# A two-layer block with routed experts: places turned with their weights in them, outputs gated as they leave, the general path moved to the end

## The chip, the cores and the metric

One core of a Trainium2 chip runs the whole program in one launch. The metric is device time in microseconds (us). Engines: PE is the matrix engine (PEld its weight loads), DVE the vector engine, ACT the scalar engine, POOL the GpSimd, SP the queue that issues nearly all loads. PE's clock is granted at one of two levels, 1.2 and 2.4 GHz; the profile gives it as a share of the higher.

## The reference, cut to what matters

256 tokens of width 1024 go through two layers. A layer has a token mixer (three branches, untouched here) and then a mixture of 16 experts in 4 groups, of which each token uses two of one group:

```
x  = x + g_a * token_mixer(...)
hf = rmsnorm(x, ffn_norm) * (1 + sc_f) + sh_f
lg, le = hf @ w_rg + b_rg, hf @ w_re + b_re            # group and expert logits
g      = argmax(lg);  top two experts inside group g   # (the first at a tie)
w2     = softmax(top two) * softmax(lg)[g]
combine[token, expert] = w2 at its two experts, else 0
hid    = silu(hf @ w_gate[e]) * (hf @ w_up[e]) * combine
x      = x + g_f * sum_e hid[e] @ w_down[e]
```

Products are float32. Weights of the dense part are split in a high and a low part (fp32r) and multiplied in three passes.

## The kernel before, in words

Tokens lie in two blocks of 128 (t = 0, 1). At the end of the mixer the w_out product comes in two halves of columns (hf) and two blocks. For each, `residual` (L1046) adds to x, sums its squares on ACT (L1055), turns it on PE (L1059) and multiplies it with the router's weights (L1068). `logits` (L1072) makes the norm's factor and the logits, and on ACT the high part xh of the normed tokens (L1081). `place` (L1084) finds the two experts of each token on DVE in a chain of small passes that ends in E (L1092), counts on PE which place the token gets among its expert's (L1095), and writes the place matrix Sm (L1102): token by expert by 32 places, one where the token sits. Behind it come the low parts xl, on DVE (L1105). The residual of block 1, half 1, is ordered behind E of block 0 (L1053).

`gather` (L1112) multiplies xh and xl with Sm: each expert gets a block of 2 x 32 token places. Each result is moved from PSUM by ACT, or by DVE for every second one of block 1.

Experts go in eight pairs q, two at once on the two halves of PE's columns. `gate_up(q)` (L1185) is 32 matmul instructions on four loads of 1 MB; `hidden` (L1199) makes silu times up on DVE and multiplies with cs[:, q], the weight of the token at each place; `turned_hidden` (L1207) turns that on PE, ACT copies it; `down` (L1215) is 16 instructions in two halves of columns on two more loads, and `split` (L108) writes its result as a high part on ACT and a low part on DVE (L109). `scatter` (L1291) multiplies the turned places ST with these two parts, in PSUM sums acc[t][hf] over all experts. PE's order in the loop is gate_up(q+1), scatter(q-1), down(q), turn of q+1; `queued` (L1179) fixes it.

Between gate_up(0) and gate_up(1) stand: the count of tokens that found no place (L1261), the weights by place, as 32 instructions that multiply Sm's columns with the combine weights (L1276) and two copies to cs (L1279), and 16 transposes of Sm (L1284), four to a PSUM bank, copied to ST by ACT (L1285). The combine weights come from DVE and ACT (Exp at L1237, L1238, then L1239 on), in free gaps that the scheduler finds.

`overfull` (L375) is the general path for tokens without a place: a branch on a flag, not taken with this input. It stands before down(7); every engine reads the flag (L377) and branches (L378). In its body it adds to acc.

`last_add` (L1326) multiplies acc by the gate g_f (rows[:, 1]) and adds it to x: in layer 0 inside the next layer's norm (L436), in layer 1 before the stores (L1335).

Loads: `pump` (L203) takes them in one fixed order whenever a buffer is put back to one of the pools wa, fs, rs; SP issues them in that order.

## Time and profile before

| | us |
|---|---|
| median of 3 runs | 837.86 (836.51 to 838.67) |
| profiled execution | 837.31 |
| its span, first to last instruction | 835.5 |
| PE busy | 788.2 (94%) |
| DVE busy | 539.5 (65%) |
| ACT busy | 387.0 (46%) |
| POOL busy | 30.0 (4%) |

The experts' part runs from 304.3 to 420 in layer 0 and from 714.6 to 829 in layer 1. A row of the timeline has its start, its length, the engine, the line, what is written and read, the count, and in brackets the idle time before it and what ended it. A row of a table by stretches has its limits, its length, the busy time (and count) of PE, PEld, DVE, ACT and POOL, the granted clock, the share of the DMA engines and GB/s. A row by lines has the busy time, the mean of one in ns, and the idle time before.

### The profile page before, as it was taken

Reading aid. Unit: us, or ns where it says so; the run is one execution under the profiler, and the core shown is the slowest. Engines: PE = TensorE matmul, PEld = TensorE weight load, DVE = VectorE, ACT = ScalarE, POOL = GpSimd, SP = SyncE. Lnnn points to the kernel's source line nnn. Section 1 sums busy time; section 2 is a strip of 40 time slices with the busy share of each in tenths; the row PEclk is TensorE's granted clock in tenths of the full one; section 3 lists DMA queues with packets and bytes.
Section 4 is the critical chain, followed back from the end, with each engine's and each line's share of the span. In section 5 each row is a group of like instructions: output and inputs, shape, how many; then the busy total and the mean of one; then the engine's idle time right before and its main releaser. Section 6 shows DMA issues by size and latency. Waiting matters only on the chain. (4 is left out here: it accounts for less than half of the span.)

```text
span 835.5 us, 11106 instructions
## 1 busy us (share of the span) xinstructions
PE 788.2 (94%) x3836; PEld 550.4 (66%) x3836; DVE 539.5 (65%) x1384; ACT 387.0 (46%) x855; POOL 30.0 (4%) x60
## 2 busy tenths in 40 slices
PE   4999999999999889999869999999999997999996
PEld 2876877788887755333358687887888885633332
DVE  6889889888999641111288987998557757211113
ACT  5477747654455242111267674776555444311111
POOL 0103001000000000000000300000000000000001
PEclk9999999999999988999979998999999997899999
DMA  9975745789899558999726366668977446599981
GB/s 340 407 299 167 269 169 200 310 312 374 320 416 371 197 198 343 422 420 422 283 108 231 115 270 249 214 244 318 356 264 254 142 152 252 201 370 420 420 349 51
DMA packets 36109, 234.37 MB, mean 281 GB/s; under 512 B 4017, under 2 KB 4689, under 8 KB 10450
## 3 DMA queue, kind: packets, MB, share of 16 engines
q1 hardware_dynamic: 35410, 231.52, 71.9%
q0 software_dynamic: 576, 2.10, 0.7%
q8 instruction: 31, 0.51, 0.2%
q14 instruction: 28, 0.23, 0.1%
q10 hardware_dynamic: 64, 0.02, 0.0%
HBM read 232.55 MB, written 1.06 MB: 280 GB/s over the span
## 5 line engine op out<-in xcount | busy, mean ns | idle before, releaser
L472 PE MATMUL mm<-rs,rs 128*128 128x512 f32 (+1 forms) x432 | 173.2, 404 | 5.5 <-ACT rs L563 4.9
L365 ACT ACTIVATE rs<-wa 128x512 fp32r<-128x512 f32 (+1 forms) x224 | 135.4, 633 | 90.9 <-PE mm L473 68.9
L473 PE MATMUL mm<-rs,rs 128*128 128x512 f32 (+1 forms) x432 | 175.2, 406 | 0.1
L474 PE MATMUL mm<-rs,rs 128*128 128x512 f32 (+1 forms) x432 | 174.8, 405 | 0.0
L365 DVE TENSOR_TENSOR rs<-wa,rs 128x512 fp32r<-128x512 f32 (+1 forms) x224 | 148.5, 682 | 39.3 <-ACT rs L365 25.0
L284 DVE SCALAR_TENSOR_TENSOR wa<-wa,cb 128x1024 f32<-128x1024 f32 x90 | 107.9, 1214 | 0.0
L472 PEld LDWEIGHTS mm<-rs,rs 128*128 128x128 f32 x432 | 82.9, 193 | 22.3 <-ACT rs L563 6.2
L473 PEld LDWEIGHTS mm<-rs,rs 128*128 128x128 f32 x432 | 83.6, 194 | 16.7 <-DVE rs L564 1.1
L474 PEld LDWEIGHTS mm<-rs,rs 128*128 128x128 f32 x432 | 83.7, 194 | 15.7 <-issue 1.4
L1203 DVE SCALAR_TENSOR_TENSOR th<-th,mm 128x256 f32<-128x256 f32 x16 | 6.7, 421 | 98.2 <-ACT th L1202 98.1
L109 DVE TENSOR_TENSOR fs<-mm,fs 128x512 fp32r<-128x512 f32 x32 | 22.1, 691 | 63.6 <-ACT fs L109 63.6
L1195 PE MATMUL mm<-wa,xs 128*64 128x512 f32 x160 | 58.5, 603 | 0.0
L1195 PE MATMUL mm<-fs,xs 128*64 128x512 f32 x192 | 58.3, 603 | 0.0
L1202 ACT ACTIVATE th<-mm 128x256 f32<-128x256 f32 x16 | 6.1, 384 | 105.6 <-PE mm L1195 105.6
L109 ACT ACTIVATE fs<-mm 128x512 fp32r<-128x512 f32 x32 | 19.1, 597 | 69.8 <-PE mm L1224 69.8
L1195 PE MATMUL mm<-rs,xs 128*64 128x512 f32 x160 | 42.8, 595 | 0.0
L472 PE MATMUL mm<-rs,xs 128*128 128x512 f32 x96 | 37.6, 392 | 0.0
L474 PE MATMUL mm<-rs,xs 128*128 128x512 f32 x96 | 37.5, 391 | 0.0
L473 PE MATMUL mm<-rs,xs 128*128 128x512 f32 x96 | 37.4, 390 | 0.0
L1195 PEld LDWEIGHTS mm<-wa,xs 128*64 128x64 f32 x160 | 17.2, 139 | 29.7 <-issue 29.7
L1224 PE MATMUL mm<-fs,hid 128*64 128x512 f32 x104 | 32.8, 598 | 1.6 <-DVEq L378 1.6
L365 ACT ACTIVATE rs<-fs 128x512 fp32r<-128x512 f32 x40 | 23.8, 627 | 21.0 <-PE mm L473 14.8
(334 smaller groups left out, 1309.3 us busy)
## 6 DMA issues: line engine op xcount, KB each, us to landing
wa<-in_ws_dram SPq DMA_DIRECT2D x83, 1024.0 KB, 7.0
fs<-in_ws_dram SPq DMA_DIRECT2D x47, 1024.0 KB, 10.2
wa<-in_wada_dram SPq DMA_DIRECT2D x40, 1024.0 KB, 5.0
rs<-in_ws_dram SPq DMA_DIRECT2D x30, 1024.0 KB, 12.3
wa<-in_wada_dram SPq DMA_DIRECT2D x10, 512.0 KB, 10.5
wa<-in_ws_dram SPq DMA_DIRECT2D x6, 512.0 KB, 8.8
fs<-in_wada_dram SPq DMA_DIRECT2D x6, 512.0 KB, 9.7
fs<-row POOLq DMA_DIRECT2D x4, 512.0 KB, 6.9
```

The source lines that it names most:

```text
L109: return ACT.activation(h, src, AF.Copy), DVE.tensor_tensor(l, src, h.bitcast(F32), op=OP.subtract)
L284: DVE.scalar_tensor_tensor(w, w, 0.5, cb, op0=OP.mult, op1=OP.mult, accum_out=mods[l][:, 2 * i + j:2 * i + j + 1])
L365: pinned(ACT.activation(h[:, cs_], r[:, cs_], AF.Copy), DVE.tensor_tensor(lo[:, cs_], r[:, cs_], h[:, cs_].bitcast(F32), op=OP.subtract))
L472: PE.matmul(o, ah[:, kb + k, ts], hv[:, k], start=st, stop=False)
L473: PE.matmul(o, al[:, kb + k, ts], hv[:, k], start=False, stop=False)
L474: PE.matmul(o, ah[:, kb + k, ts], lv[:, k], start=False, stop=en)
L1195: queued(PE.matmul(pgu[64 * i:64 * i + 64], a, wv[i][:, k], start=kb == 0, stop=kb == 7))
L1202: ACT.activation(th, pgu[:, :256], AF.Tanh, scale=0.5)
L1203: DVE.scalar_tensor_tensor(th, th, 1.0, pgu[:, :256], op0=OP.add, op1=OP.mult)
L1224: queued(PE.matmul(py[hf][i_], hid_[:, f, i_], wv[i][:, f, hs], start=f == 0, stop=f == 1))
```

## The change

The weight matmuls go. Sm holds only the block's own places and lies in the buffer that ST takes later (so it is taken earlier, before place(0)); a second matrix Sw, Sm times the combine weights with the zeros of the other block, is made on DVE and turned. A sum over a row of the turned matrix is the weight at that place (cs), and a comparison with zero gives ST. Four transposes make one group; groups 0 and 1 stand between gate_up(0) and gate_up(1), groups 2 and 3 and the count behind gate_up(1) and the turn of hidden 0. `down` multiplies its result by the gate before it is split, into the row buffer of the other gate, and `last_add` only adds. `overfull` comes after the last scatter; in its body the down weights are multiplied by the gate. The low parts of block 0 are made by an ACT copy and a GpSimd subtraction. The first two passes of the combine weights are ordered behind the low parts of block 1.

```diff
-        def overfull(acc, cov, ovi):
+        def overfull(acc, cov, ovi, gate):
...
+                    for f in range(2):
+                        DVE.tensor_tensor(wv[:, f], wv[:, f], gate, op=OP.mult)
...
-        xh_s, xl_s, sm_s = (fs.get(F32R) for _ in range(3))
+        xh_s, xl_s = (fs.get(F32R) for _ in range(2))
+        sw_s = fs.get()
...
-        Sm = sm_s.rearrange("p (t e u s) -> p t e u s", t=2, e=16, u=2)
+        Sw = sw_s.rearrange("p (t e u s) -> p t e u s", t=2, e=16, u=2)
         for t in range(2):
-            POOL.memset(Sm.bitcast(F32)[:, t, :, 1 - t], 0.0)
+            POOL.memset(Sw[:, t, :, 1 - t], 0.0)
...   # logits
             for hs in halves:
                 ACT.activation(xh[:, t, hs], x[:, t, hs], AF.Copy, scale=r)
+            if t == 0:
+                for hf, hs in enumerate(halves):
+                    xn = tm_s[:, 1024 * hf:1024 * hf + 512]
+                    ACT.activation(xn, x[:, t, hs], AF.Copy, scale=r)
+                    POOL.tensor_tensor(xl[:, t, hs], xn, xh[:, t, hs].bitcast(F32), op=OP.subtract)
...   # place
-            for hs in halves:
-                o = DVE.scalar_tensor_tensor(xl[:, t, hs], x[:, t, hs], rstd[t], xh[:, t, hs].bitcast(F32), ...)
-                behind_of(o, placed)
+            if t:
+                for hs in halves:
+                    o = DVE.scalar_tensor_tensor(xl[:, t, hs], x[:, t, hs], rstd[t], xh[:, t, hs].bitcast(F32), ...)
+                    behind_of(o, placed)
+                order["xl"] = o
...
         logits(0)
-        place(0)
         for s, kb, hv, lv in todo:
             mm3(ps[1], kb, 8, hv, lv, mh, ml, 1)
             rs.put(s)
         rs.put(mh_s, ml_s)
+        st_s = rs.get()
+        Sm = st_s[:, :1024].rearrange("p (t e s) -> p t e s", t=2, e=16)
+        ST = st_s.rearrange("p (q t n) -> p q t n", q=8, t=2)
+        place(0)
         residual(1, 1, ps[1])
         logits(1)
-        xs.put(tm_s, hT_s)
+        xs.put(hT_s, tm_s)
         gather(0, 0, 4)
         place(1)
         gather(0, 4)
-        st_s = rs.get()
-        ST = st_s.rearrange("p (q t n) -> p q t n", q=8, t=2)
...   # down
-                split(y_s[:, hs], y_s[:, 1024 + 512 * hf:1536 + 512 * hf], py[hf])
+                y = rows_s[:, hs]
+                DVE.tensor_tensor(y, py[hf], rows[:, 1, hs], op=OP.mult)
+                split(y_s[:, hs], y_s[:, 1024 + 512 * hf:1536 + 512 * hf], y)
...
-        pgu = gate_up(0)
+        pgs = [gate_up(0)]
...   # both first passes of the combine weights
+        behind_of(DVE.tensor_tensor(ex, ...), order["xl"])
+        behind_of(DVE.tensor_tensor(d, ...), order["xl"])
...
+        for t in range(2):
+            DVE.tensor_tensor(Sw[:, t, :, t], Sm[:, t].bitcast(F32), cmb[:, t, :, None].to_broadcast([128, 16, 32]), op=OP.mult)
+        cs = small("cs", 8)
+
+        def turned_places(g):
+            p = mmt("sm").rearrange("p (q t n) -> p q t n", q=2, t=2)
+            for i in range(2):
+                for t in range(2):
+                    e = 2 * (2 * g + i)
+                    queued(PE.transpose(p[:, i, t], Sw[:, t, e:e + 2].rearrange("p e u s -> p (e u s)"), ident))
+            g2 = slice(2 * g, 2 * g + 2)
+            DVE.tensor_reduce(cs[:, g2], p.rearrange("p q t n -> p q (t n)"), axis=AX.X, op=OP.add)
+            DVE.tensor_scalar(ST[:, g2], p, 0.0, None, op0=OP.is_gt)
+
+        for g in range(2):
+            turned_places(g)
+        pgs.append(gate_up(1))
+        hid = turned_hidden(hidden(0, pgs[0]), pgs[0])
+        for g in range(2, 4):
+            turned_places(g)
         pcn = mmt("sm")[:, :16]
         for t in range(2):
-            PE.matmul(pcn, ones, c2[:, t], start=t == 0, stop=t == 1)
+            queued(PE.matmul(pcn, ones, c2[:, t], start=t == 0, stop=t == 1))
...   # gone: L1273 to L1285, the weight matmuls, cs, transposes and ACT copies
-        fs.put(sm_s)
+        fs.put(sw_s)
         pump()
...   # scatter: t outside, hf inside
-        hid = turned_hidden(hidden(0, pgu), pgu)
         for q in range(8):
             if q < 7:
-                pgu = gate_up(q + 1)
+                pgu = gate_up(q + 1) if q else pgs[1]
...
             else:
                 xs.put(*xg_s)
-                overfull(acc, covf, ovi)
-                last.clear()
                 down(hid, ys[q % 2])
                 scatter(q - 1, ys[(q - 1) % 2])
         scatter(7, ys[1])
+        overfull(acc, covf, ovi, rows[:, 1])
...
         if l == depth - 1:
-            y_s = fs.get()
-            for hf in range(2):
-                for t in range(2):
-                    last_add(acc, rows_s, t, hf, y_s[:, 1024 * t:1024 * t + 1024], DVE if hf else POOL)
+            for t in range(2):
+                for hf in range(2):
+                    last_add(acc, t, hf)
                     store(t, hf)
-            fs.put(y_s)
...
-    def last_add(acc, rows_s, t, hf, y, eng=DVE):
+    def last_add(acc, t, hf):
         hs = slice(512 * hf, 512 * hf + 512)
-        y = y[:, 512 * hf:512 * hf + 512]
-        DVE.tensor_tensor(y, acc[t][hf], rows_s[:, 1024 + 512 * hf:1536 + 512 * hf], op=OP.mult)
-        eng.tensor_tensor(x[:, t, hs], x[:, t, hs], y, op=OP.add)
+        DVE.tensor_tensor(x[:, t, hs], x[:, t, hs], acc[t][hf], op=OP.add)
```

## Rows read from the trace of the kernel before

**Rows 1.** The page: busy shares, and one line of its costliest groups.

```profile
PE 788.2 (94%) x3836; PEld 550.4 (66%) x3836; DVE 539.5 (65%) x1384; ACT 387.0 (46%) x855; POOL 30.0 (4%) x60
...
L109 DVE TENSOR_TENSOR fs<-mm,fs 128x512 fp32r<-128x512 f32 x32 | 22.1, 691 | 63.6 <-ACT fs L109 63.6
```

**Rows 2.** Stretches of the span: length, busy us (count) by engine, clock, DMA.

```profile
311.30:327.70 16.40, 16.40 (x90) 10.75 (x90) 1.61 (x7) 3.05 (x6) 0.00 (x0) 0.79 0.83 321
327.70:412.40 84.70, 82.04 (x369) 30.56 (x365) 17.10 (x30) 13.85 (x30) 0.10 (x1) 1.00 1.00 412
...
721.60:738.00 16.40, 16.40 (x90) 11.22 (x90) 1.62 (x7) 3.05 (x6) 0.00 (x0) 0.79 0.82 318
```

**Rows 3.** Timeline of PE: four transposes in layer 0, a steady gate/up in layer 1.

```profile
280.71 0.63 PE L1059 MATMUL sm<-cst,fs 128*128 128x128 f32 x4
...
806.55 0.44 PE L1210 MATMUL mm<-cst,th 128*128 128x128 f32 x2
...
813.94 2.11 PE L1296 MATMUL sm<-fs,rs 128*128 128x512 f32 x8
```

**Rows 4.** Finer stretches of layer 0, columns as in rows 2.

```profile
294.10:296.50 2.40, 0.00 (x0) 0.00 (x0) 1.34 (x13) 2.01 (x5) 0.00 (x0) 0.93 1.01 427
...
315.60:319.80 4.20, 4.20 (x20) 3.88 (x20) 1.44 (x6) 2.10 (x4) 0.00 (x0) 0.50 0.95 398
319.80:322.10 2.30, 2.30 (x7) 0.77 (x8) 0.00 (x0) 0.57 (x2) 0.00 (x0) 0.57 0.67 175
```

**Rows 5.** Groups by line from 304 to 330, busy us and mean ns.

```profile
L1276 PE MATMUL sm<-cmb,fs 128*128 128x2 f32 x32 | 4.1, 264 | 0.0
...
L1284 PEld LDWEIGHTS sm<-cst,fs 128*128 128x128 f32 x16 | 3.5, 238 | 0.0
```

**Rows 6.** Timeline around the branch, before down(7) of layer 0 and layer 1.

```profile
409.96 0.38 ACT L1212 ACTIVATE hid<-mm 128x256 f32<-128x256 f32 x1
...
412.40 0.61 PE L1224 MATMUL mm<-wa,hid 128*64 128x512 f32 x1 [2.66 <-DVEq L378]
...
820.24 0.38 ACT L1212 ACTIVATE hid<-mm 128x256 f32<-128x256 f32 x1
...
821.61 3.65 PE L1224 MATMUL mm<-fs,hid 128*64 128x512 f32 x16 [1.61 <-DVEq L378]
```

**Rows 7.** Timeline of logits and placing, layer 0, and one wait in layer 1.

```profile
283.90 1.34 ACT L1081 ACTIVATE fs<-fs,rstd 128x512 fp32r<-128x512 f32 x2 [2.58 <-DVE rstd L123]
...
288.98 1.41 DVE L1105 SCALAR_TENSOR_TENSOR fs<-fs,rstd,fs 128x512 fp32r<-128x512 f32 x2
...
297.75 1.41 DVE L1105 SCALAR_TENSOR_TENSOR fs<-fs,rstd,fs 128x512 fp32r<-128x512 f32 x2
...
706.32 0.16 DVE L1239 TENSOR_REDUCE psel<-ex 128x2 f32<-128x8 f32 x1 [2.53 <-ACT ex L1237]
```

**Rows 8.** Timeline of the tails of layer 0 and layer 1.

```profile
415.98 3.92 PE L1296 MATMUL sm<-fs,rs 128*128 128x512 f32 x16
...
423.52 0.15 DVE L438 TENSOR_TENSOR msx<-ss 128x1 f32<-128x1 f32 x1
...
825.20 3.96 PE L1296 MATMUL sm<-fs,rs 128*128 128x512 f32 x16
...
829.96 2.71 SPq L1335 DMA_DIRECT2D out_dram<-fs  x4
```

**Rows 9.** Line L1331: ns of one, least, median and most, with first and last start.

```profile
L1331 DVE TENSOR_TENSOR fs<-fs,fs x6: 677/680/1468, 419.8 to 831.6; 128x512 f32<-128x512 f32 x6
...
L1331 POOL TENSOR_TENSOR fs<-fs,fs x2: 1257/1263/1269, 828.7 to 829.9; 128x512 f32<-128x512 f32 x2
```

**Rows 10.** Expert loads (L241, layer 0): landing times; an issue; its first use.

```profile
DMA to landing us min/median/max: 4.8/13.7/19.6
...
374.72 3.82 SPq L241 DMA_DIRECT2D fs<-in_ws_dram  x3
...
399.71 0.14 PEld L1195 LDWEIGHTS mm<-fs,xs 128*64 128x64 f32 x1
```

More of the change, by code (lines that the diff above doesn't have):

```diff
@@ L435, in normed @@
                 if tail:
-                    last_add(*tail, t, hf, xn[:, t], DVE)
+                    last_add(tail[0], t, hf)
                 ACT.activation(xn[:, t, hs], x[:, t, hs], AF.Square, accum_out=ss[:, hf:hf + 1])
@@ L1101, in place @@
             DVE.tensor_tensor(pl16[:, t], pl16[:, t], pp, op=OP.add)
-            placed = DVE.tensor_tensor(Sm[:, t, :, t], iota[:, None, :32].to_broadcast([128, 16, 32]),
+            placed = DVE.tensor_tensor(Sm[:, t], iota[:, None, :32].to_broadcast([128, 16, 32]),
                                        pl16[:, t, :, None].to_broadcast([128, 16, 32]), op=OP.is_equal)
-            for hs in halves:
-                o = DVE.scalar_tensor_tensor(xl[:, t, hs], x[:, t, hs], rstd[t], xh[:, t, hs].bitcast(F32), op0=OP.mult, op1=OP.subtract)
-                behind_of(o, placed)
+            if t:
+                for hs in halves:
+                    o = DVE.scalar_tensor_tensor(xl[:, t, hs], x[:, t, hs], rstd[t], xh[:, t, hs].bitcast(F32), op0=OP.mult, op1=OP.subtract)
+                    behind_of(o, placed)
+                order["xl"] = o
         xg_s = []
@@ L1119, in gather @@
                 p = mmt("sm").rearrange("p (e s) -> p e s", e=16)
-                o = PE.matmul(p, xh[:, t, ks], Sm[:, t, :, t], start=True, stop=False)
+                o = PE.matmul(p, xh[:, t, ks], Sm[:, t], start=True, stop=False)
                 if t == k == 0:
@@ L1124, in gather @@
                     behind_of(o, order["p"])
-                o = PE.matmul(p, xl[:, t, ks], Sm[:, t, :, t], start=False, stop=True)
+                o = PE.matmul(p, xl[:, t, ks], Sm[:, t], start=False, stop=True)
                 if k == 3 and not t:
@@ L1234, in layer @@
         ohg = o1[:, :, 0]
-        DVE.tensor_tensor(ex, lg[:, :, 0:4], m1[:, :, 0:1].to_broadcast([128, 2, 4]), op=OP.subtract)
-        DVE.tensor_tensor(d, m2, m1[:, :, 1:5], op=OP.subtract)
+        behind_of(DVE.tensor_tensor(ex, lg[:, :, 0:4], m1[:, :, 0:1].to_broadcast([128, 2, 4]), op=OP.subtract), order["xl"])
+        behind_of(DVE.tensor_tensor(d, m2, m1[:, :, 1:5], op=OP.subtract), order["xl"])
         ACT.activation(ex, ex, AF.Exp)
@@ L1264, in layer @@
         DVE.tensor_copy(ovi[:, 0:1], ovf[:, 0:1])
-        covf = cov.rearrange("p e t -> p (e t)")
-        Smf = Sm.bitcast(F32)
-        def places(p, t):
-            return Smf[:, t, 2 * p:2 * p + 2].rearrange("p e u s -> p (e u s)")
-        pcs = mmt("sm")[:, :16].rearrange("p (q i) -> p q i", q=8)
-        for p_ in range(8):
-            for t in range(2):
-                PE.matmul(pcs[:, p_], places(p_, t), cmb[:, t, 2 * p_:2 * p_ + 2], start=t == 0, stop=t == 1)
-        cs = small("cs", 8)
-        for i in range(2):
-            DVE.tensor_copy(cs[64 * i:64 * i + 64], pcs[64 * i:64 * i + 64, :, i])
-        for q in range(4):
-            p = mmt("sm").rearrange("p (q t n) -> p q t n", q=2, t=2)
-            for i in range(2):
-                for t in range(2):
-                    PE.transpose(p[:, i, t], places(2 * q + i, t), ident)
-            ACT.activation(ST[:, 2 * q:2 * q + 2], p, AF.Copy)
-        fs.put(sm_s)
+        fs.put(sw_s)
         pump()
@@ L1291, in scatter @@
         def scatter(q, y_s):
-            for hf in range(2):
-                for t in range(2):
+            for t in range(2):
+                for hf in range(2):
                     for a in range(2):
@@ L1317, in layer @@
         if l == depth - 1:
-            y_s = fs.get()
-            for hf in range(2):
-                for t in range(2):
-                    last_add(acc, rows_s, t, hf, y_s[:, 1024 * t:1024 * t + 1024], DVE if hf else POOL)
+            for t in range(2):
+                for hf in range(2):
+                    last_add(acc, t, hf)
                     store(t, hf)
-            fs.put(y_s)
         return acc, rows_s
-    def last_add(acc, rows_s, t, hf, y, eng=DVE):
+    def last_add(acc, t, hf):
         hs = slice(512 * hf, 512 * hf + 512)
-        y = y[:, 512 * hf:512 * hf + 512]
-        DVE.tensor_tensor(y, acc[t][hf], rows_s[:, 1024 + 512 * hf:1536 + 512 * hf], op=OP.mult)
-        eng.tensor_tensor(x[:, t, hs], x[:, t, hs], y, op=OP.add)
+        DVE.tensor_tensor(x[:, t, hs], x[:, t, hs], acc[t][hf], op=OP.add)
     def store(t, hf):
```

1 line of the change is left out of this document (added).

## The prediction

> **What bounds the kernel now.** I read the busy shares first: the matrix engine, PE, is busy for 94% of the span [rows 1], so a gain has to come out of PE's own work or out of a place where PE waits. Next the table by stretches, cut at the stages that the diff touches. In each layer 16.40 us lie between the last gate/up product of expert pair 0 and the first down product of that pair, with PE busy throughout but at a mean clock of 0.79; in the 84.70 us behind it PE has 82.04 us of work at full clock [rows 2]. The reader is to see that the first stretch is long for what it must do. It holds one gate/up product (7.39 us with the turn of a hidden block, from L1210 to the next scatter, in the steady part [rows 3]); the rest is the block that the change rewrites. The finer cut shows how it hurts: the clock is 0.50 while the places are transposed and still 0.57 in the first 2.3 us of the next gate/up [rows 4]. By line, the weight matmuls L1276 alone are 4.1 us and the loads of the transposes L1284 3.5 us [rows 5]. Then the waits, in the timeline: PE stands still before the last down product until DVE is past the branch L378 [rows 6], and it has no work from 294.1 to 296.5 [rows 4], where DVE waits for ACT's Exp in the middle of block two's placing [rows 7].
>
> **The change part by part.** The working is against the profiled execution: 837.31 us, a span of 835.50 and 1.81 around it. It lies 0.55 under the median shown (837.86).
>
> *1. Places and weights.* Gone: 32 matmul instructions a layer (L1276), the two copies behind them, and the position of the 16 transposes in front of gate_up(1). New order on PE: gate_up(0), 8 transposes, gate_up(1), turn of hidden 0, 8 transposes, the overflow count, down(0). Four transposes take 0.63 us at full clock, their tail included [rows 3]; eight in a row I take as 1.0 and not 1.26, since one tail stands for both fours. So: 1.0 + 7.39 + 1.0 + 0.5 (four small products at L1276's 4.1/32) + 0.15 for changes of tile = 10.05 us where 16.40 stood: 6.3 us a layer, 12.6 in both. The lower end: all 16 transposes at the pace of L1284 (3.5 us instead of 2.0) and a slow restart as in 319.8 to 322.1 (0.43 of 2.3 us, 1.0), which leaves 3.8 a layer; the upper, transposes with no tails, 6.6. I take the value near the top, because the clock fell only after some 4 us of L1276's two-column products, and the new block has dense products 1 to 2 us away on either side. What DVE gets instead (two multiplications for Sw, four sums and four comparisons, ten passes of 0.69 us by L109's row [rows 1]) lies beside gate_up(0) and gate_up(1), 7 us each; the pieces for pair 0 are wanted only behind gate_up(1).
>
> *2. The branch leaves the place before down(7).* There PE waits until DVE has drained and branched. ACT has the hidden block at 410.34 and 820.62, PE starts at 412.40 and 821.61 [rows 6]: 2.06 and 0.99 us. After the change PE waits for ACT's copy alone. But ACT's second copy of the outputs, 0.6, now waits for a DVE multiplication of 0.69; if it keeps its place ahead of the hidden block, that much is given back. Bounds 1.37 to 2.06 and 0.30 to 0.99; between them I take 1.6 and 0.5, together 2.1.
>
> *3. The tail.* Each output add loses its multiplication: four DVE passes instead of eight, and nothing left for GpSimd. But acc is also an output of the branch body, so the first add waits until PE is past the branch, behind its last scatter product; now DVE starts its multiplications while PE still scatters. Layer 0: PE ends at 419.90, DVE starts the norm at 423.52, 3.62 later [rows 8]; after, 0.3 for the branch and four adds at some 0.65 give 2.9: 0.7 to 0.8 gained. Layer 1: PE ends at 829.16, the last store is issued within the row that ends at 832.67, some 3.2 behind PE; after, 2.9: 0.3 gained. Sum 1.1. The pass that gates the outputs is new in front of the last scatter; it is covered by scatter(6), eight of the 16 products of 3.96 us [rows 8]. If that cover is short, 0.7 per layer is lost, and if the branch itself shows, another 1 to 2. Bounds -3 to +1.5 for both.
>
> *4. Norm and placing.* Block one's low parts, 1.41 us of DVE right before block two's norm [rows 7], go to ACT and GpSimd; the Exp inputs go behind block two's low parts, so that DVE no longer stands waiting for ACT (2.53 us in layer 1) with E still to make. If nothing opposed it, PE's gap of 2.4 us would shrink by 1.4 in layer 0 and 2.5 in layer 1. Against it: GpSimd needs 1.26 us for such a subtraction, and a DVE add with both inputs in SBUF that met one took 1468 ns, not 680 [rows 9]. ACT's copies for GpSimd end some 0.67 us behind L1081, at about 285.9 [rows 7], so the two subtractions cover 285.9 to 288.5. In just that time DVE makes E of block one, with such inputs, and the second residual is ordered behind E. A wait of 0.8 us (one meeting) to 2.5 (two whole instructions) lands on that chain, where 1.41 was saved. I take +0.2 in layer 0, +0.9 in layer 1, where more waiting on Exp goes, and take off 0.3 a layer for Exp now queueing with ACT's evictions of the second gather: +0.5. Bounds -3 and +3.9.
>
> The Trainium skill, page "SBUF — State Buffer", section "Who interferes with whom", says that a VectorE instruction with two SBUF inputs and a GpSimd instruction that reads SBUF exclude each other for a whole instruction, whichever came first. The trace agrees, with its 1468 ns. By that rule in its strictest form part 4 would be about -1 and the total 823.0; without any exclusion, +3.3 and 818.7.
>
> *5. Gating the outputs as they leave.* 16 DVE passes of 0.69 [rows 1], 11 us a layer, in a stage where DVE is busy for 17.10 of 84.70 us [rows 2]; PE wants an output only one gate/up later. The PSUM bank is free after one pass instead of two. Nothing but the ends in parts 2 and 3.
>
> *6. Loads.* PE runs 6.6 us ahead in layer 0. A load for gate_up(7) issued at 374.72 landed by 394.3 at the latest (19.6, the longest landing) and was first used at 399.71 [rows 10]: 5.4 us to spare. It is issued when PE frees a buffer, so earlier too; the queue has room for that in the stretch before, at a share of 0.83 over 16.40 us, but none behind it (1.00) [rows 2]. Zero, and up to 1.2 us late if no load moves.
>
> Sum: 12.6 + 2.1 + 1.1 + 0.5 = 16.3. 837.31 - 16.3 = 821.0, and with the 0.55 to the median 821.5 us.
>
> **The rivals.**
> *Slow clock stays* (13%). Two pieces of transposes pull the clock down where one did. For it: 0.50 in that stretch [rows 4]. Against: the weight matmuls that stood before it are gone. Part 1 is 7.6 instead of 12.6: 826.5.
> *Weights late* (7%). The change does not do what it says, because PE waits for Sw in front of the first transposes: Exp, some 15 small DVE passes and two of 0.69 now begin behind block two's low parts and share ACT and DVE with the second gather. Counted from the end of those low parts (299.2 now [rows 7]): 2.5 for Exp, 3.0 for the small passes at 0.2, 3.2 for four evictions and 1.4 for Sw give 309.3 in layer 0, 2 us ahead of the end of gate_up(0) at 311.3 [rows 2]. If it comes 5 us later than that in each layer, 6 us are lost: 827.5.
> *The tail costs* (5%). The branch, no longer under the experts' products, is paid in the open with the longer output chain: part 3 is -3, 825.6.
> *GpSimd in nobody's way* (10%). Part 4 at +3.3: 818.7.
> *Loads become the bound* (5%), the slower side. The expert stage already moves 412 GB/s at a share of 1.00 [rows 2]. The places' buffer is freed only behind gate_up(1), and the queue of loads is one line in program order: a load that waits for a late buffer holds all behind it. For a loss, each layer has to wait more than 8.2 us for weights, that is, loads must land some 7 us later than they do now, three loads' worth. Against: they are issued by buffers that PE frees earlier. Then 840.
>
> **How the numbers follow.** The forecast has 60%, its time is 821.5. The range holds the forecast, GpSimd free, and most of the clock, weights and tail cases: 816.5 to 828.5. What a measurement can tell from no change is about 0.3%, 2.5 us: only loads, or several misfortunes at once, come that near to 837.86. Faster 0.92, same 0.03, slower 0.05.
>
> **What would show it.** Right: about 10 us between gate_up(0) and down(0) in both layers with the clock near 1; no wait on L378 before down(7); DVE's first output add within 0.5 us of PE's last scatter; DVE passes of 0.8 us and more beside GpSimd's two subtractions in the placing, and E of block one later than now. Wrong: a clock of 0.5 at the new transposes, PE waiting for Sw or for a load, or a long record of L378 in the tail.

## The result, and the profile after

The changed kernel takes 816.0 us, median of four (815.1 to 821.2), beside 838.3 for the kernel before (836.5 to 839.1): a ratio of 0.975, 95% interval 0.971 to 0.979. The forecast was 821.5 with a range from 816.5 to 828.5, worked from a median of 837.86. The ratio puts that at 816.9, just inside the range; the median of 816.0 itself lies 0.5 below its lower end. The profiled execution spans 813.3 us where the one before spanned 835.5.

First the page of the changed kernel, its busy shares; they answer to [rows 1]. The matrix engine has 16 us less to do and a slightly higher share; DVE has 29 us more, nearly all of it where PE does not wait.

```profile
PE 772.1 (95%) x3772; PEld 535.4 (66%) x3772; DVE 568.4 (70%) x1422; ACT 385.7 (47%) x851; POOL 32.9 (4%) x62
```

Next the stretches of the changed kernel, columns as in [rows 2]: the end of gate_up(0) to down(0), down(0) to down(7), and finer, the first eight transposes and the first 2.3 us of gate_up(1) behind them, which answer to [rows 4]; last, layer 1.

```profile
309.60:319.20 9.60, 9.60 (x56) 4.60 (x54) 4.22 (x9) 1.10 (x3) 0.00 (x0) 1.00 1.01 424
319.20:401.85 82.65, 82.12 (x367) 30.63 (x366) 25.60 (x47) 13.17 (x26) 0.10 (x1) 1.00 0.98 408
309.60:310.60 1.00, 1.00 (x10) 0.84 (x8) 0.46 (x2) 0.38 (x1) 0.00 (x0) 1.00 1.04 426
310.60:312.90 2.30, 2.30 (x13) 0.87 (x14) 2.30 (x5) 0.00 (x0) 0.00 (x0) 1.00 0.99 417
...
707.48:717.08 9.60, 9.60 (x56) 4.61 (x54) 4.22 (x9) 1.10 (x3) 0.00 (x0) 1.00 1.01 422
```

The stretch of 16.40 us at a mean clock of 0.79 is now 9.60 at 1.00, in both layers. Gate_up(1) starts at full clock, with 13 products in 2.3 us where 7 were counted before.

In front of down(7), the timeline of layer 0 and layer 1 (start, duration, engine, in brackets the idle time and its releaser); [rows 6] had 2.66 and 1.61 us behind the branch:

```profile
401.42 0.38 ACT L1224 ACTIVATE hid<-mm 128x256 f32<-128x256 f32 x1 [0.72 <-PE mm L1222]
...
401.85 0.64 PE L1236 MATMUL mm<-wa,hid 128*64 128x512 f32 x1 [0.53 <-ACT hid L1224]
...
402.12 0.63 ACT L109 ACTIVATE fs<-fs 128x512 fp32r<-128x512 f32 x1 [0.32 <-DVE fs L1238]
...
799.73 0.64 PE L1236 MATMUL mm<-wa,hid 128*64 128x512 f32 x1 [0.53 <-ACT hid L1224]
```

ACT's second output copy (402.12) now stands behind the hidden block (401.42); only the 0.53 us for that block are left.

The tails, for [rows 8]: timeline of layer 0, then layer 1.

```profile
405.44 4.24 PE L1312 MATMUL sm<-fs,rs 128*128 128x512 f32 x16
...
407.51 0.68 DVE L109 TENSOR_TENSOR fs<-fs,fs 128x512 fp32r<-128x512 f32 x1
...
409.86 2.48 DVE L1341 TENSOR_TENSOR fs<-fs,sm 128x512 f32<-128x512 f32 x4 [1.67 <-PEq L378]
...
415.02 0.47 PE L339 MATMUL sm<-cst,fs 128*128 128x128 f32 x1 [5.34 <-ACT fs L445]
...
803.32 4.08 PE L1312 MATMUL sm<-fs,rs 128*128 128x512 f32 x16
...
807.58 2.48 DVE L1341 TENSOR_TENSOR fs<-fs,sm 128x512 f32<-128x512 f32 x4 [1.67 <-PEq L378]
```

The first output add starts 0.18 us behind PE's last scatter product in both layers, released by PE's queue at the branch L378 and not by a sum. The last scatter takes 4.24 and 4.08 us, not 3.92 and 3.96: its fourth product waits for the low part of the gated right half, which ends at 408.2.

Last the placing of layer 0, for [rows 7] and [rows 9]: GpSimd's two subtractions, and DVE beside them.

```profile
284.18 2.49 POOL L1089 TENSOR_TENSOR fs<-xs,fs 128x512 fp32r<-128x512 f32 x2 [24.16 <-ACT xs L1088]
284.19 1.29 DVE L1044 TENSOR_TENSOR o<-o,revt 128x16 f32<-128x16 f32 x1
285.51 0.17 DVE L1046 TENSOR_REDUCE fm<-o 128x4 f32<-128x16 f32 x1
285.72 0.98 DVE L1047 TENSOR_TENSOR o<-o,fm 128x16 f32<-128x16 f32 x1
286.73 0.17 DVE L1099 TENSOR_TENSOR E<-o,o 128x16 f32<-128x16 f32 x1
```

Two DVE steps of 0.18 us take 1.29 and 0.98 us and end 0.03 us after a GpSimd subtraction ends (285.45 and 286.67). The reduction between them, with one input, takes its usual 0.17 in the middle of the second.

**Where 22.2 us of span went**, from marks in the two timelines (the first record of each step on PE or DVE):

| stretch | before | after | gained | forecast |
|---|---|---|---|---|
| start to residual(0,1), layer 0 | 279.14 | 277.38 | 1.8 | 0 |
| residual(0,1) to gate_up(0), layer 0 / 1 | 25.19 / 26.76 | 25.18 / 25.19 | 0.0 + 1.6 | 0.5 |
| gate_up(0) to down(0) | 23.35 / 23.33 | 16.65 / 16.66 | 6.7 + 6.7 | 12.6 |
| down(0) to down(7) | 84.72 / 83.65 | 82.64 / 82.64 | 2.1 + 1.0 | 2.1 |
| down(7) to the last scatter's end | 7.51 / 7.55 | 7.83 / 7.67 | -0.3 - 0.1 | 1.1 with the next |
| from there to the first transpose of layer 1 / to the end | 6.36 / 6.38 | 5.34 / 5.94 | 1.0 + 0.4 | |
| layer 1, first transpose to residual(0,1) | 261.61 | 260.23 | 1.4 | 0 |

The first and the last line are 3.1 us from code that the change leaves as it was.

### The profile page after: what moved, and what is told of

It is laid out like the page before. It is cut to its first block, busy times and chain, and to the rows that moved or that the text cites. A ratio compares the mean times of both kernels' runs of the same rounds, so it can differ in the third digit from the quotient of the medians.

```text
span 813.3 us, 11024 instructions
## 1 busy us (share of the span) xinstructions
PE 772.1 (95%) x3772; PEld 535.4 (66%) x3772; DVE 568.4 (70%) x1422; ACT 385.7 (47%) x851; POOL 32.9 (4%) x62
## 5 line engine op out<-in xcount | busy, mean ns | idle before, releaser
L365 ACT ACTIVATE rs<-wa 128x512 fp32r<-128x512 f32 (+1 forms) x224 | 135.3, 633 | 87.9 <-PE mm L475 63.3
L365 DVE TENSOR_TENSOR rs<-wa,rs 128x512 fp32r<-128x512 f32 (+1 forms) x224 | 148.5, 683 | 38.2 <-ACT rs L365 25.4
L1207 PE MATMUL mm<-wa,xs 128*64 128x512 f32 x168 | 64.4, 595 | 0.0
L1207 PE MATMUL mm<-fs,xs 128*64 128x512 f32 x184 | 60.8, 595 | 0.0
L109 ACT ACTIVATE fs<-fs 128x512 fp32r<-128x512 f32 x32 | 20.2, 630 | 68.2 <-DVE fs L1238 68.2
L1238 DVE TENSOR_TENSOR fs<-mm,fs 128x512 f32<-128x512 f32 x32 | 22.0, 688 | 32.8 <-PE mm L1236 32.8
L1236 PE MATMUL mm<-wa,hid 128*64 128x512 f32 x80 | 36.5, 599 | 1.1 <-ACT hid L1224 1.1
L1207 PEld LDWEIGHTS mm<-wa,xs 128*64 128x64 f32 x168 | 19.1, 137 | 26.9 <-issue 26.6
L1236 PE MATMUL mm<-fs,hid 128*64 128x512 f32 x96 | 36.5, 598 | 0.0
```

Source lines behind the costliest of these rows:

```text
L109: return ACT.activation(h, src, AF.Copy), DVE.tensor_tensor(l, src, h.bitcast(F32), op=OP.subtract)
L365: pinned(ACT.activation(h[:, cs_], r[:, cs_], AF.Copy), DVE.tensor_tensor(lo[:, cs_], r[:, cs_], h[:, cs_].bitcast(F32), op=OP.subtract))
L1207: queued(PE.matmul(pgu[64 * i:64 * i + 64], a, wv[i][:, k], start=kb == 0, stop=kb == 7))
L1236: queued(PE.matmul(py[hf][i_], hid_[:, f, i_], wv[i][:, f, hs], start=f == 0, stop=f == 1))
L1238: DVE.tensor_tensor(y, py[hf], rows[:, 1, hs], op=OP.mult)
```

## The experiments

Theory: the change gained 19 us in the stretches that it rewrites, above all because nothing pulls the clock down between gate_up(0) and down(0); the GpSimd part is a loss; and the 3.1 us are the clock's chance (only in part borne out, see below). Every experiment changes the changed kernel (but for the last). The marks, columns "placing": residual(0,1) to gate_up(0); "pair 0": gate_up(0) to down(0); "last scatter": down(7) to its end; "tail": from there to layer 1's first transpose / to the end; "untouched": the first and the last line of the table above. Layer 0 / layer 1 each. The ratio is to the runs of the kernel before on the same chip (medians 841.0, 840.8 and 838.7 us in the three groups of runs).

| run | median us | ratio, 95% | placing | pair 0 | last scatter | tail | untouched |
|---|---|---|---|---|---|---|---|
| changed, again | 816.2 | 0.969 to 0.977 | 24.6 / 25.1 | 16.65 / 16.65 | 7.84 / 7.65 | 5.34 / 5.94 | 277.2 / 261.6 |
| low parts on DVE | 812.8 | 0.963 to 0.974 | 23.4 / 23.5 | same | 7.82 / 7.66 | same | 281.8 / 260.3 |
| Exp early | 817.1 | 0.970 to 0.977 | 24.6 / 25.3 | same | 7.84 / 7.66 | same | 279.2 / 257.3 |
| low parts behind the norm | 811.8 | 0.963 to 0.970 | 22.5 / 23.0 | same | 7.84 / 7.66 | same | 279.0 / 258.9 |
| weight products back | 825.4 | 0.979 to 0.988 | 24.6 / 24.6 | 21.87 / 21.90 | 7.82 / 7.66 | same | 277.1 / 260.4 |
| transposes together | 817.9 | 0.971 to 0.979 | 24.7 / 25.2 | 16.84 / 16.84 | 7.84 / 7.65 | same | 280.3 / 257.3 |
| branch before down(7) | 822.1 | 0.975 to 0.982 | 24.9 / 25.1 | same | 9.25 / 7.64 | 3.78 / 4.31 | 277.2 / 261.2 |
| gating at the end | 822.1 | 0.973 to 0.981 | 24.7 / 25.1 | same | 7.51 / 7.51 | 7.43 / 7.93 | 279.1 / 262.0 |
| low parts on DVE, Exp early | 822.5 | 0.978 to 0.984 | 25.3 / 24.6 (see below) | 18.31 / 18.31 | 7.82 / 7.66 | same | 277.8 / 263.7 |
| low parts behind norm, scatter turned | 811.9 | 0.963 to 0.972 | 22.7 / 22.9 | same | 7.51 / 7.51 | same | 281.8 / 261.5 |
| no general path | 813.7 | 0.966 to 0.972 | 25.1 / 25.2 | same | 7.84 / 7.66 | 3.65 / 4.61 | 281.8 / 260.3 |
| before, again (one run) | 838.7 | | 25.2 / 26.8 | 23.36 / 23.32 | 7.51 / 7.53 | 6.36 / 6.37 | 280.4 / 261.7 |

**Is the gain in untouched code the change's?** The changed kernel and the kernel before, unedited.

> The changed kernel as it is, once more. Theory A: 3.1 us of the 22.2 us by which the profiled span shrank come from TensorE's granted clock in code that the change does not touch: 1.7 us ahead of residual(0, 1) of layer 0, where the kernel before shows a clock of 0.50 from 114 to 116 us and the changed one 1.00, and 1.4 us in the first products of layer 1 (0.50 from 430 to 434 us before). Such stretches come and go from run to run, so the runs of one and the same kernel should lie some 1 to 6 us apart, as one of the four times of the changed kernel (821.2 against 815.1 to 816.1) suggests, and this trace may show a slow stretch at another place. Median 816.0 plus or minus 1.5. Theory B: the change itself keeps the clock up at these two places, the first by some shift in the loads ahead of it, the second by the shorter pause of TensorE between the layers; then this trace repeats the first one within 0.5 us at every mark, with clock 1.00 from 114 to 116 us and the first products of layer 1 again near full clock.

> The kernel before, one more profile. Theory A (the clock in the attention stage and at the start of layer 1 is chance): residual(0, 1) of layer 0 comes anywhere from 277 to 282 us, not again at 279.1; the steps that the change touches repeat within 0.5 us: residual(0, 1) to gate_up(0) 25.2 and 26.8 us, gate_up(0) to the first down product 23.3 us in both layers, the pause in front of down(7) 2.7 and 1.6 us. Rival (the kernel before always loses 1.7 us there): 279.1 us again.

The stretches of the kernel before, then of the changed kernel and of its repeat, all in the attention of layer 0; then of the run with the low parts on DVE, whose code is the same there.

```profile
112.00:114.00 2.00, 2.00 (x14) 1.50 (x12) 1.83 (x7) 0.47 (x2) 0.00 (x0) 0.89 0.00 0
114.00:116.00 2.00, 2.00 (x8) 1.49 (x6) 1.58 (x6) 0.59 (x3) 0.00 (x0) 0.50 0.33 45
```

```profile
114.00:116.00 2.00, 2.00 (x10) 1.36 (x9) 1.98 (x6) 1.55 (x4) 0.00 (x0) 1.00 0.29 45
```

```profile
114.00:116.00 2.00, 2.00 (x9) 1.34 (x8) 1.96 (x6) 1.55 (x4) 0.00 (x0) 1.00 0.34 53
```

```profile
114.00:116.00 2.00, 2.00 (x5) 1.15 (x4) 1.65 (x5) 1.26 (x4) 0.00 (x0) 0.50 0.44 66
...
120.00:122.00 2.00, 2.00 (x6) 1.49 (x6) 1.74 (x4) 0.00 (x0) 0.00 (x0) 0.50 0.85 356
```

Over the fourteen traces residual(0,1) of layer 0 comes between 277.1 and 281.8 us, and this goes with the slow stretch at 114 us: 277.1 to 277.8 in the five traces without it, 279.0 to 280.4 in the six where it is over by 120 us, 281.8 in the three where the clock is still 0.50 from 120 to 122. Of the ten edited runs seven have it, and what they edit lies behind it. Layer 1's untouched stretch takes 257.3 to 263.7 us, and 261.6 in the repeat of the changed kernel, as in the kernel before. So swings of this size need no edit, as theory A says; the changed kernel alone ran from 814.7 to 822.3. Two things keep it from being shown that the whole 3.1 us are chance. The repeat came without the stretch at 114 us again, at 277.2, as theory B had it for this place; and both traces of the kernel before have it. And over all runs on record the kernel before has a mean of 839.5 us (37 runs) and the changed kernel 817.2 (10 runs): 22.3 us apart, with a standard error of 1.0, where the edited stretches account for 19.1 us in the first pair of traces and 19.7 in the second. Whether the change also keeps the clock up more often in code that it does not edit stays open. The two traces of the kernel before agree to 0.1 us in every stretch that the change touches. From here on the marks decide where a time differs by less than 3 us.

**What the low parts on GpSimd do.**

```diff
-            if t == 0:
-                for hf, hs in enumerate(halves):
-                    xn = tm_s[:, 1024 * hf:1024 * hf + 512]
-                    ACT.activation(xn, x[:, t, hs], AF.Copy, scale=r)
-                    POOL.tensor_tensor(xl[:, t, hs], xn, xh[:, t, hs].bitcast(F32), op=OP.subtract)
...
-            if t:
-                for hs in halves:
+            for hs in halves:
```

> The changed kernel, with block one's low parts made by VectorE again (two passes of 0.7 us behind block one's places, as before the change), and everything else as changed: the inputs of Exp still behind block two's low parts. Theory A (GpSimd's work costs on VectorE what it saves): block one's E comes 1.9 us earlier, since the two comparisons that took 1293 and 979 ns beside GpSimd take some 175 ns again, the low parts put 1.4 back, and gate_up(0) starts up to 0.5 us earlier in each layer, counted from residual(0, 1): 815.0 us, between 814.5 and 816.5. Rival (the low parts on GpSimd are what shortened the placing of layer 1 by 1.6 us): 1.4 us are lost in each layer, 818.8 us. Second rival (TensorE's own products bound this stretch): 816.0 us.

The line of the comparison L1044, ns of one (least, median, most), in the changed kernel and then with the low parts on DVE:

```profile
L1044 DVE TENSOR_TENSOR o<-o,revt x8: 174/180/1293, 282.9 to 692.1; 128x20 f32<-128x20 f32 x4, 128x16 f32<-128x16 f32 x4
```

```profile
L1044 DVE TENSOR_TENSOR o<-o,revt x8: 174/177/182, 287.4 to 693.1; 128x20 f32<-128x20 f32 x4, 128x16 f32<-128x16 f32 x4
```

Residual(0,1) to E of block one takes 9.6 to 9.7 us in the changed kernel and 7.80 without GpSimd's subtractions, in both layers. Block two's E, which the second gather waits for, comes 1.1 to 1.7 us earlier in layer 0 and 1.6 to 1.7 in layer 1, and the placing is as much shorter: 1.2 to 1.8 us and 1.6. That is more than theory A's half microsecond, and 812.8 us lies below its range. The offload saved 1.4 us behind block one's E and lost 1.8 to 1.9 in front of it, on a chain that PE waits for. Rival one, that it pays, is out; so is the second, that PE's own products bound this stretch.

**Where they cost least.** Here block one's low parts go behind the last step of block two's norm:

```diff
+            if t:
+                for hs in halves:
+                    o = DVE.scalar_tensor_tensor(xl[:, 0, hs], x[:, 0, hs], rstd[0], xh[:, 0, hs].bitcast(F32), op0=OP.mult, op1=OP.subtract)
+                    behind_of(o, last_r)
...
```

> The changed kernel with block one's low parts on VectorE, but behind the last step of block two's norm, where VectorE waits for TensorE's logits (1.17 us in layer 0 of the changed kernel). Theory A (the exclusion with GpSimd is a loss of 1.9 us on the chain through E, the two passes are covered by the wait for the logits): block two's norm starts 1.9 us earlier than in the changed kernel, the logits' combination 1 us or more earlier, and gate_up(0) starts 0.5 to 1.5 us earlier in each layer: 814.0 us, between 813 and 815.5. Rival (the gather needs the low parts as soon as the logits are done, so TensorE waits for these two passes): 816.0 to 817.5 us.

Its timeline in layer 0:

```profile
289.60 1.07 PE L1071 MATMUL sm<-wrs,xs 128*128 128x20 f32 x8 [0.69 <-ACT xs L1067]
...
290.73 1.41 DVE L1084 SCALAR_TENSOR_TENSOR fs<-fs,rstd,fs 128x512 fp32r<-128x512 f32 x2
...
292.06 0.23 DVE L1086 SCALAR_TENSOR_TENSOR lg<-sm,rstd,lrow 128x20 f32<-128x20 f32 x1
```

The two passes begin as PE ends the logits, so they cost DVE about 1.2 us here and are not covered as theory A had it; but block two's norm no longer stands behind them. The placing is 22.5 / 23.0 us, 2.1 less than the changed kernel's repeat in both layers: 811.8 us against 816.2, more than theory A's range gave. Block two's E comes 1.2 and 1.7 us earlier; the rest lies behind it, and its cause was not isolated.

**The order of Exp.** Freed from its place behind block two's low parts, first in the changed kernel (the line for `ex` likewise):

```diff
-        behind_of(DVE.tensor_tensor(d, m2, m1[:, :, 1:5], op=OP.subtract), order["xl"])
+        DVE.tensor_tensor(d, m2, m1[:, :, 1:5], op=OP.subtract)
```

> The changed kernel without the order that puts the two subtractions for Exp behind block two's low parts; they may go into VectorE's queue among the steps of block two's first maxima, as before the change. Theory A (this order is what shortened layer 1's placing): VectorE waits for ScalarE's Exp with E still to make, 0.8 to 2.5 us; gate_up(0) starts 0.5 us later in layer 0 and 1.6 us later in layer 1, together 818.1 us, between 817 and 819.5. Rival (the low parts on GpSimd are what shortened it; the order is worth nothing): 816.0 us within 0.5, though VectorE shows the wait.

Theory A missed: 24.6 / 25.3 us, as in the changed kernel. The rival's wait did not show either: DVE never waited, because only the two subtractions moved; the reduction that reads Exp stayed behind the low parts. So this run says nothing of what the wait costs. With the low parts on DVE as well, both edits together, it does not stay:

> The changed kernel with both halves of its fourth part undone: block one's low parts on VectorE as before, and the inputs of Exp no longer behind block two's low parts. Here the reduction that reads Exp stands between the last two steps of block two's E in VectorE's queue, as in the kernel before; with Exp freed alone it stayed behind the low parts, so that run did not bring the wait back. Theory A (the wait for Exp is what the change took away in layer 1, and the exclusion with GpSimd ate what the offload saved): residual(0, 1) to gate_up(0), 23.4 and 23.5 us with the low parts alone on VectorE, becomes 25.2 us in layer 0 and 26.8 in layer 1, as in the kernel before; about 5 us slower than with the low parts alone on VectorE, 818 us. Rival (the order is worth nothing, as the run with Exp freed seemed to say; something else in the new order of the places shortened layer 1): 23.4 and 23.5 us as there, 813 us.

DVE in layer 1 of that run:

```profile
696.66 0.17 DVE L1094 TENSOR_TENSOR E<-o,o 128x16 f32<-128x16 f32 x1
697.80 0.16 DVE L1247 TENSOR_REDUCE psel<-ex 128x2 f32<-128x8 f32 x1 [0.97 <-ACT ex L1245]
...
697.98 0.17 DVE L1095 TENSOR_TENSOR E<-E,o 128x16 f32<-128x16 f32 x1
```

E waits again, 0.71 us in layer 0 and 0.97 in layer 1. In the kernel before it was 0.99 and 2.53 us; [rows 7] has the second, and this is the first:

```profile
296.04 0.16 DVE L1239 TENSOR_REDUCE psel<-ex 128x2 f32<-128x8 f32 x1 [0.99 <-ACT ex L1237]
```

Block two's E comes 0.8 and 1.1 us later than with Exp behind, so the rival is out for that much. PE also took the first two gate products ahead of the last part of the gather, so the whole is counted from residual(0,1) to down(0): 43.6 / 42.9 us against 40.0 / 40.2, 3.6 and 2.7 more (822.5 us, beyond theory A's 818). The other 2.8 and 1.6 us lie behind E. There PE gathered at a clock of 0.50 for 5.5 us in layer 0 and 3.4 in layer 1, and near 1.00 in the run with Exp behind (a stretch of layer 0 in this run, then in that one):

```profile
298.00:300.30 2.30, 2.30 (x7) 1.77 (x6) 0.18 (x3) 2.13 (x4) 0.00 (x0) 0.50 0.02 6
```

```profile
298.20:305.23 7.03, 6.54 (x26) 4.31 (x26) 4.77 (x10) 6.97 (x12) 0.00 (x0) 1.00 0.45 186
```

The kernel before gathers at 0.50 too, from 297.9 to 301.3 us; that the order of Exp brings this about is not shown.

**Why pair 0 is faster.** The small products back, in front of the transposes, into a bank that nobody reads; then all transposes in one piece.

```diff
+        pcs = mmt("sm")[:, :16].rearrange("p (q i) -> p q i", q=8)
+        for p_ in range(8):
+            for t in range(2):
+                queued(PE.matmul(pcs[:, p_], Sw[:, t, 2 * p_:2 * p_ + 2].rearrange("p e u s -> p (e u s)"),
+                                 cmb[:, t, 2 * p_:2 * p_ + 2], start=t == 0, stop=t == 1))
         for g in range(2):
             turned_places(g)
```

> The changed kernel with 32 two-column products a layer put back in front of the first eight transposes (the weighted places against the weights, into a bank that nobody reads; the outputs do not change). Theory A (it is these small products that pull TensorE's clock down, and what follows pays for it): they take 3.8 to 4.1 us a layer themselves, the transposes behind them and the start of gate_up(1) show a granted clock of 0.50 again, and gate_up(0) to gate_up(1), 8.04 us in the changed kernel, becomes 13.5 to 15 us: 11 to 14 us in both layers, 828 to 830 us. Rival (their own time is all they cost): 8.04 becomes 11.8 to 12.2 us with a clock of 1.00 behind them, 824 us.

Stretches of layer 0 of that run: the products, eight transposes, the start of gate_up(1).

```profile
309.00:312.40 3.40, 3.40 (x32) 3.40 (x33) 0.42 (x1) 0.25 (x1) 0.00 (x0) 1.00 1.00 419
312.40:313.40 1.00, 1.00 (x11) 0.83 (x12) 0.41 (x1) 0.00 (x0) 0.00 (x0) 0.93 1.05 442
313.40:316.00 2.60, 2.60 (x8) 0.75 (x10) 2.46 (x5) 0.00 (x0) 0.00 (x0) 0.50 1.01 419
```

The products hold PE for 3.6 us a layer, and gate_up(0) to gate_up(1) becomes 11.6 us: that is the rival's number, not theory A's 13.5 to 15. But the clock falls to 0.50 behind the transposes, which the rival excluded, and this costs 1.65 us from the start of gate_up(1) on: 5.2 us a layer of the 6.7 that the rewriting gained. So theory A is right that there is a fall and too high in its cost, and 825.4 us lies between the two. The other 1.5 us a layer was not isolated; in the kernel before, all sixteen transposes stood behind the products, at 0.50 [rows 4].

```diff
-        for g in range(2):
+        for g in range(4):
             turned_places(g)
         pgs.append(gate_up(1))
...
-        for g in range(2, 4):
-            turned_places(g)
```

> The changed kernel with all sixteen transposes of the places in one piece in front of gate_up(1), none behind it. Theory A (transposes of this kind do not pull the clock down; cutting them in two is worth nothing): the clock stays at 1.00, gate_up(0) to gate_up(1) grows from 8.04 us to 9.0 to 9.3, gate_up(1) to the first down product shrinks from 8.61 by as much, and the sum of 16.65 us stays within 0.4: 816.2 us. Rival (a piece of sixteen lets the clock fall as in the kernel before): the sum becomes 17.5 to 19 us a layer, 818 to 821 us. Second rival (sixteen need the weights of all pairs no sooner, but the sums and comparisons on VectorE delay the turned hidden block): up to 1 us a layer more, at full clock.

The sum is 16.84 instead of 16.65 us, at a clock of 1.00 (two rows of that run, the transposes and what follows):

```profile
312.10:314.00 1.90, 1.90 (x20) 1.73 (x18) 1.36 (x3) 0.38 (x1) 0.00 (x0) 1.00 1.03 436
314.00:316.00 2.00, 2.00 (x11) 0.75 (x12) 2.00 (x5) 0.00 (x0) 0.00 (x0) 1.00 0.98 406
```

Sixteen transposes in a row do not pull the clock down here; with the two-column products in front of eight it falls. The transposes took 1.9 us and the products 3.6, so whether their kind or the length of the stretch without dense products decides was not separated. Cutting the transposes in two is worth 0.2 us a layer.

**The branch.** Back in front of down(7), and then left out with the path behind it.

```diff
                 xs.put(*xg_s)
+                overfull(acc, covf, ovi, rows[:, 1])
+                last.clear()
                 down(hid, ys[q % 2])
                 scatter(q - 1, ys[(q - 1) % 2])
         scatter(7, ys[1])
-        overfull(acc, covf, ovi, rows[:, 1])
```

> The changed kernel with the branch on overflow back in front of the last pair's down products. Theory A (the wait in front of down(7) comes back, but the output adds no longer wait for the branch and start while TensorE still scatters, block one's four products being first): the pause in front of down(7), 0.53 us in both layers of the changed kernel, becomes 2.0 us in layer 0 and 1.0 in layer 1, 2.0 us lost; of the four adds only the last is left behind the last scatter product, so that scatter's end to the next layer's first transpose falls from 5.34 us to 3.5, and scatter's end to the end of the span from 5.94 to 4.1: 3.7 us gained. Net 1.7 us faster than the changed kernel, 814.5 us. Rival (the place of the branch is what gained, the tail does not care): 2.0 us slower, 818.2 us. Second rival (ScalarE's squares and the norm bound the tail of layer 0, the store's latency that of layer 1): the tail gains 1 us or less, 817 us.

Layer 0 of that run:

```profile
404.36 0.93 PE L1236 MATMUL mm<-wa,hid 128*64 128x512 f32 x1 [3.48 <-DVEq L378]
...
412.24 2.48 DVE L1342 TENSOR_TENSOR fs<-fs,sm 128x512 f32<-128x512 f32 x4
```

A miss, 822.1 us for 814.5. The tail did what theory A said: the adds start 1.4 us ahead of the last scatter's end (413.61), and it is 1.6 us shorter in both layers. But the pause is 3.48 and 2.69 us and not 2.0 and 1.0. DVE, which PE waits for, now has a gating pass of pair 6 to make before ACT can copy its result and DVE can make the low part; then comes, in layer 0 as before the change, a split of weights of the next layer (L365, 1.10 us), and only then does DVE branch. And in layer 0 the products behind the pause run at half the clock, so that down(7) to the last scatter's end takes 9.25 us for 7.84:

```profile
404.40:407.90 3.50, 3.50 (x10) 1.32 (x12) 0.00 (x0) 0.00 (x0) 0.00 (x0) 0.52 0.97 391
```

```diff
         scatter(7, ys[1])
-        overfull(acc, covf, ovi, rows[:, 1])
```

> The changed kernel with the branch and the general path behind it left out (an overfull expert's surplus tokens would be lost): what the branch costs where the change put it. Theory A (the output adds wait for the branch, not for the sums): TensorE's last scatter product to the next layer's first transpose falls from 5.34 to 3.8 us and to the end of the span from 5.94 to 4.3, as with the branch in front of the last down products, and the pause in front of down(7) stays 0.53 us: 3.2 us less, 812.8 us. Rival (the branch costs nothing here; the adds and the norm behind them are the tail): within 0.3 us in both places, 816 us. Second rival (also the code behind the branch costs a load of instructions): another 1 to 2 us less, 811 us.

Theory A: 1.7 and 1.3 us less in the tails, the pause unchanged. That is what the branch and the code behind it cost together at the end of a layer; the further 1 to 2 us of the second rival did not come. With the gating on the way out, the place in front of down(7) costs 3.0 and 2.2 us in the pause.

**The gating.** Undone: multiplications at the end again, two adds on GpSimd in layer 1.

```diff
-                DVE.tensor_tensor(y, py[hf], rows[:, 1, hs], op=OP.mult)
-                split(y_s[:, hs], y_s[:, 1024 + 512 * hf:1536 + 512 * hf], y)
+                split(y_s[:, hs], y_s[:, 1024 + 512 * hf:1536 + 512 * hf], py[hf])
...
+        DVE.tensor_tensor(y, acc[t][hf], rows_s[:, 1024 + 512 * hf:1536 + 512 * hf], op=OP.mult)
+        eng.tensor_tensor(x[:, t, hs], x[:, t, hs], y, op=OP.add)
```

> The changed kernel with the outputs gated as before: no multiplication on the way out of the down products, eight passes (multiply and add) at the end of each layer, two of the last four adds on GpSimd. Theory A: behind the branch block one's norm waits for four passes in place of two, 1.3 us more from scatter's end to the next layer's first transpose (5.34 to 6.6 us); in layer 1 the last store comes 1.5 to 2.5 us later (5.94 to 7.9 us); the last scatter no longer waits for a gated output, 0.3 us back in layer 0: 819 us, between 818 and 820. Rival (sixteen gating passes a layer weigh on the expert stage, from the first to the last down product 82.64 us): that stretch shrinks by 1 us or more, and the kernel is as fast as the changed one.

The tails grow by 2.1 and 2.0 us, the last scatter gives back 0.3 and 0.15, the expert stage is 82.8 us instead of 82.6. Theory A, with more in layer 0's tail than expected; the marks come to 4 us, and the time, 822.1 us, lies above its range.

**A better version.** The low parts behind the norm, and in the last pair the left halves of both blocks first:

```diff
-            for t in range(2):
-                for hf in range(2):
+            for t, hf in ((0, 0), (1, 0), (0, 1), (1, 1)) if q == 7 else ((0, 0), (0, 1), (1, 0), (1, 1)):
```

> A version that ought to beat both: block one's low parts on VectorE behind block two's norm, and in the last pair alone the scatter takes the left half of both blocks before the right half, so that the third product no longer waits for the gated right half. Expected: the last down product to the last scatter product's end falls from 7.82 to 7.5 us in layer 0 and from 7.66 to 7.5 in layer 1, with the tail as long as before, because its first add waits for the branch and so for the last scatter product in either order: 0.5 us less than with the low parts behind the norm alone, 811.3 us. Rival (the adds start with block one's halves, so that turning the scatter makes them later): the tail grows by 0.6 us a layer, 812.5 us.

Its scatter in layer 0:

```profile
407.40 3.92 PE L1312 MATMUL sm<-fs,rs 128*128 128x512 f32 x16
...
411.51 0.69 DVE L1341 TENSOR_TENSOR fs<-fs,sm 128x512 f32<-128x512 f32 x1 [1.35 <-PEq L378]
```

The last scatter ends 0.3 and 0.15 us sooner and the tail is as long as before, as expected. In the time it can't be seen (806.8 to 818.5 us). Both versions with the low parts behind the norm lie near 812 us, a ratio of 0.967 (0.963 to 0.970 the one, 0.963 to 0.972 the other) to the kernel before, and below the changed kernel's 0.973 (0.969 to 0.977). The intervals still touch; that the first of them is faster rests on its placing, 2.1 us shorter in each layer.

## Why the prediction was right

All four signs that it named for being right stand in the rows above. Part by part:

1. *Places and weights*: forecast 12.6, measured 13.4 us. About 10 us was forecast for the new stretch and 9.60 came, at a clock of 1.00. The step that the value stood on, that the clock falls with the two-column products and not with the transposes alone, is shown by the two runs above, though not whether the products' kind or their length does it.
2. *The branch*: forecast 1.6 and 0.5 in front of down(7), measured 2.1 and 1.0. The step mis-sized is ACT's copy: 0.6 us was allowed for keeping its place ahead of the hidden block, and it lost that place, because it now waits for DVE's multiplication.
3. *The tail*: forecast 1.1, measured 1.0, out of larger pieces than foreseen; that they cancel to the forecast is luck. Gating at the outputs is worth 2.1 and 2.0 us in the tails; the branch at the end takes 1.7 and 1.3 back. The prediction saw that the adds would wait for PE at the branch (0.18 us behind it), and sized it as one sum. Its warning that the cover of the last gating pass might be short came true for 0.3 and 0.1 us.
4. *Norm and placing*: forecast 0.5, measured 1.6, and here two larger terms of opposite sign were hidden; that the sum came within 1.1 us is luck. Counted with the low parts on DVE in both kernels, the rest of the new order shortens the placing by 1.8 and 3.2 us (25.19 to 23.4, 26.76 to 23.5), and GpSimd takes 1.2 to 1.8 and 1.6 back. Of the 1.8 and 3.2, block two's E brings 1.1 and 2.6, which is what DVE waited for Exp in the kernel before, 0.99 and 2.53; the prediction counted that wait in layer 1 alone. The other 0.7 and 0.6 lie behind E and were not isolated. The prediction's bounds for the meeting, 0.8 to 2.5 us on E's chain, hold: 1.93. The Trainium skill, page "SBUF — State Buffer", section "Who interferes with whom", says that such a pair excludes each other for a whole instruction, and that a DVE instruction with at most one SBUF input does not meet GpSimd, outside the modes in which DVE uses two ports. This trace agrees on both: 1.29 and 0.98 us for the steps with two inputs, ending with GpSimd's, and 0.17 for the reduction between them. The prediction's strict form of the rule (part 4 at -1) fell on another term: the rest of the order gained 1.8 and 3.2 us with the low parts still on DVE, where 1.4 and 2.5 was the most that it gave to the whole part.
5. *Gating in the expert stage and the loads*: forecast 0, measured 0. From gate_up(2) to gate_up(7) of layer 0 both kernels take 65.07 us, and a load for gate_up(7) of the changed kernel, issued at 367.1, lands at 387.1, 4.6 us ahead of the product that reads it; the forecast had 5.4 for the kernel before.

The sum of the parts is 16.3 in the forecast and 19.1 us in the marks; the 3.1 us left of the profiled difference are the clock in code that was not edited, for which the forecast had no term; how much of it is chance stays open. None of the rivals came: the clock stays up, the weighted places are ready 3 us ahead of the transposes, PE waits for no load, and GpSimd is in somebody's way.

## What to carry to other kernels

Move work to GpSimd only where the vector engine, for as long as it takes, has no step with two SBUF inputs on the critical chain; otherwise find the place in the vector engine's own queue where the next step waits anyway. Look for products of a few columns: here they cost twice, 3.6 us in their weight loads and 1.65 us in the clock of the dense products behind them. Before you explain a gain of half a per cent, cut both traces at the same marks and see whether it lies in code that was edited at all.

## What the runs showed of the hardware

- The granted clock in unedited code moved the same mark by up to 4.8 us between executions (277.1 to 281.8 us), with a stretch at 0.50 at 114 us that came in nine of fourteen traces, and in three of them was still there at 120 us.
- Thirty-two two-column products are no slower than their weight loads (3.6 of 3.7 us busy), and the clock fell to 0.50 only a microsecond behind them, under the dense products that followed (0.93 in that microsecond, 0.50 in the 2.6 us after it).
- The branch, not taken to its body, cost the wait for the engines that it gathers: a pause of 3.48 and 2.69 us in front of down(7), where 0.53 stood without it, and 1.3 to 1.7 us at the end of a layer, where the output adds stood behind it (there together with the code that it jumps over).
- Beside GpSimd's two subtractions of 1.26 us, DVE steps of 0.18 us with two inputs took 1.29 and 0.98 us; a reduction with one input took its usual 0.17.
